# First feed-forward product: the third of a group's seven products ahead of the second, one weight quarter loaded at another place, activations behind the next cast

## The chip, the cores and the metric

The kernel runs on one core of one Trainium2 chip. The metric is the device time of one execution in microseconds (us). The profiler records one execution: what every engine did and when, in us from the first instruction.

## What is computed

The whole program is one block of a network: a projection of the input, two attention-like branches, a merge, a layer norm, a feed-forward part, a gate and a second layer norm, on 512 tokens of width 1024. The change touches the feed-forward part and the work just ahead of it:

```python
h = layer_norm(DEEPNORM_ALPHA * h + merged @ w_out[l], ln1_g[l], ln1_b[l])
ff = jnp.square(jax.nn.relu(h @ w_ff1[l])) @ w_ff2[l]          # w_ff1 1024 x 4096, w_ff2 4096 x 1024
r = DEEPNORM_ALPHA * h + ff
r = r + jax.nn.sigmoid(r @ w_ple_gate[l]) * (p[l] @ w_ple_proj[l])
h = layer_norm(r, ln2_g[l], ln2_b[l])
```

## The kernel before, in words

**The first feed-forward product** (`h @ w_ff1`) is cut into four groups of 1024 columns, in the order `groups = (2, 3, 0, 1)`; t counts them 0 to 3. In a group, h is a 2 x 2 block matrix (two halves of the tokens, two of the width) and the weights are the four quarters B11, B12, B21, B22 of 512 x 512. A group's eight block products are replaced by seven products P1 to P7 of sums of blocks, after Strassen and Winograd. The sums of h blocks are made once, as tiles `hc0` to `hc6`; the rows of TensorE (PE) name a product by its tile: P1 is hc0, P2 is hc1, P3 is hc6, P4 is hc2, P5 is hc3, P6 is hc4, P7 is hc5. A product is 48 matmuls of 128 x 256: each fp32 operand is split into a high and a low part (`w1h` and `w1l` for the weights), and high by high, high by low and low by high are added up.

**The sums of weight quarters** are made in place. `w1_load` brings a quarter from HBM into a tile `w1q` (issued by SP). `w1_factor` casts the quarter to `w1h` on ScalarE (ACT) and takes the rest to `w1l` on VectorE (DVE), in two halves of 128 x 1024. Behind each half of P1, P5 and P3 it issues, from GpSimd (POOL), a transfer that adds another quarter to this half in place (`accum_op=OP.add`, L887). So there are three pairs of such adding transfers in a group:

- the **P1 pair**, behind the split of B11 for P1: adds B12 to B11. P5 uses the sum.
- the **P3 pair**, behind the split of B22 for P3: adds B12 to B22. P7 uses the sum.
- the **P5 pair**, behind the split of B11 for P5: adds B22 to B11. P6 uses the sum, and DVE adds it to B21 for P4 (`w1q<-w1q`).

**The order.** `seq` lists the steps (group, product). At step k the code first splits the weights of step k+1 (`w1_factor`), then takes the result of step k-1 out of its PSUM banks (`ff1_sums`), and then issues the matmuls of step k (`ff1`, L958). In steps with `late_` the sums come ahead of the split. `queued` keeps the ACT and DVE instructions of these parts in the order of the code, and `issue_after` does so for the matmuls. Splits write into two buffers by turns, so the split for step k+1 waits until the matmuls of step k-1 have read theirs.

**Results.** `ff1_sums` copies or adds PSUM banks into four tiles C00, C01, C10, C11 (`c` in the rows), and `act` squares the ReLU of a finished one on ACT, in two instructions, into `uLH` or `uH`; C11's is one DVE instruction (`last_act`). The finished tiles of the first two groups are stored to DRAM (`spill`, issued by SP) and read back later. `w1_banks` says which two PSUM banks a product uses: `sets[0]` or `sets[3]`, by the group's parity, for P1 and P6; `sets[1]` for P2 and P5; `sets[2]` for P3, P7 and P4. P6 adds onto P1's bank and P4 onto P7's; P3 and P7 start fresh, so the one waits until the sums have read what P4 left there, the other until they have read P3.

**Places.** Quarters B11 and B22 lie in four places w80 to w83 that hold other things before. B22 of group 0 goes into w83, B22 of group 1 into w82, B11 of group 1 into w80. Before that, w82 and w83 hold the two halves of `w_ple_proj` (tile `wp`), which `ple_projection` reads in eight small products (`ppw`, stored through `pws` to `pwd`), the four of the first half (hh = 0) first. These stand on PE directly ahead of P1 of group 0.

**After it** comes the second feed-forward product (`ff2`, L1188), built in the same way, then the gate and the last norm.

Of the kernel before, what the change touches and what calls it, by code (L numbers as in the profile page):

```python
# [50 lines left out]
def f(ap):  # L51
    return ap.bitcast(F32)
# [3 lines left out]
def block_kernel(ctx: ExitStack, tc: tile.TileContext, t, out):  # L56
    nc = tc.nc
    te, ve, se, ge, sy = nc.tensor, nc.vector, nc.scalar, nc.gpsimd, nc.sync
# [22 lines left out]
    def acc(name):  # L81
        return ps_pool.tile([P, 512], F32, tag="acc", bufs=3, name=name)

    def aux(name):
        return ps_pool.tile([P, 512], F32, tag="aux", bufs=1, name=name)

    def misc(name):
        return ps_pool.tile([P, 512], F32, tag="misc", bufs=4, name=name)
# [14 lines left out]
    def gtile(name, dtype=F32R, n=None):  # L103

        if n is None:
            n = len(gplaces) % 4
            gplaces.append(n)
        return gpool.tile([P, 4, S], dtype, tag=f"g{n}", bufs=1, name=name)


    def split(src, hi, lo, lo_eng=None):
        se.copy(hi, src)
        low(lo_eng or ve, lo, src, hi)
# [11 lines left out]
    def raw_tile(shape, name):  # L125
        return rawpool.tile(shape, F32, tag="wr", bufs=3, name=name)
# [20 lines left out]
    def chunked(src):  # L147
        return src.rearrange("(k p) c -> p k c", p=P)
# [187 lines left out]
    for i in range(1, NT):  # L336
        n = (i + 1) * P
# [325 lines left out]
    def place(name, shape, dtype, n=None, pl=None):  # L663

        if n is None:
            n = len(places) % 4
            places.append(n)
        return (pl or w2).tile(shape, dtype, tag=f"w8{n}", bufs=1, name=name)

    def load_half(src, k, hh, name, lo_eng=None, pl=None, n=None):  # L670

        raw = raw_tile([P, 2, 512], name + "r")
        sy.dma_start(raw, chunked(src[k * 256:(k + 1) * 256, hh * 512:(hh + 1) * 512]))
        w = place(name, [P, 2, 2, 512], F32R, n, pl)
        split(raw, w[:, 0], w[:, 1], lo_eng)
        return w[:, 0], w[:, 1]
# [73 lines left out]
    def half_product(ps, sh, sl, ws):  # L750

        for k, (wh, wl) in enumerate(ws):
            mm = mm3(ps, sh(k), sl(k), wh, wl, k == 0, k == len(ws) - 1)
        return mm

    def blocks(ws):
        return [(wh[:, k, :], wl[:, k, :]) for wh, wl in ws for k in range(2)]
# [37 lines left out]
    def ple_inputs():  # L795
        prw = ln.tile([P, NT, PLE], F32, name="prw")
        sy.dma_start(prw, p_d.rearrange("(i p) c -> p i c", p=P))
        pT = place("pT", [P, 2, 2, S], F32R, 0)
        pTH, pTL = pT[:, 0], pT[:, 1]
        for c in range(2):  # L800
            ps = (aux, acc)[c]("pps")
            for i in range(NT):
                te.transpose(ps[:, i * P:(i + 1) * P], prw[:, i, c * P:(c + 1) * P], ident)
            split(ps, pTH[:, c, :], pTL[:, c, :])
        wp = [load_half(t["w_ple_proj"][0], 0, hh, "wp", (ge, ve)[hh], None, 2 + hh) for hh in range(2)]
        return pTH, pTL, wp

    w_ff1, w_ff2 = t["w_ff1"][0], t["w_ff2"][0]
# [2 lines left out]
    def queued(engine, op, *args, **kw):  # L811

        if engine in order_of:
            with tc.issue_after(order_of[engine].ins):
                order_of[engine] = getattr(engine, op)(*args, **kw)  # L815
        else:
            order_of[engine] = getattr(engine, op)(*args, **kw)
# [26 lines left out]
    pTH, pTL, wp = ple_inputs()  # L844
# [5 lines left out]
    P1, P2, P3, P4, P5, P6, P7 = range(7)  # L850
    B11, B12, B21, B22 = (0, 0), (0, 1), (1, 0), (1, 1)
    groups = (2, 3, 0, 1)
    w1q, pools = {}, {}

    def w1_rows(t, w):
        c = groups[t] * 1024 + w[1] * 512
        return w_ff1[w[0] * 512:(w[0] + 1) * 512, c:c + 512].rearrange("(k p) c -> p k c", p=P)

    def w1_load(t, w):

        if t >= len(groups):
            return
        e = (t + 1) % 2
        if w == B21:
            tl = pools[e].tile([P, 4, 512], F32, tag=f"x{e}", bufs=1, name="w1q")
        else:
            tl = place("w1q", [P, 4, 512], F32, (0 if w == B11 else 2) + e)
        w1q[t, w] = tl
        if loads:
            with tc.issue_after(loads[-1].ins):  # L870
                loads.append(sy.dma_start(tl, w1_rows(t, w)))
        else:
            loads.append(sy.dma_start(tl, w1_rows(t, w)))
# [5 lines left out]
    def w1_factor(t, n):  # L879

        tl = w1q[t, W1_OF[n]]
        hi, lo = (pools[1].tile([P, 4, 512], F32R, tag="w1" + x, bufs=2, name="w1" + x) for x in "hl")
        for k in (slice(0, 2), slice(2, 4)):
            queued(se, "copy", hi[:, k], tl[:, k])
            queued(ve, "tensor_sub", lo[:, k], tl[:, k], f(hi[:, k]))
            if n in W1_ADD:
                ge.dma_start(out=tl[:, k], in_=w1_rows(t, W1_ADD[n])[:, k], accum_op=OP.add)  # L887
        if n == P6:
            for k in (slice(0, 2), slice(2, 4)):
                queued(ve, "tensor_add", w1q[t, B21][:, k], w1q[t, B21][:, k], tl[:, k])  # L890
        return hi, lo
# [11 lines left out]
    def ple_projection(i, hh):  # L903
        ps = acc("ppw")
        tok = slice(i * P, (i + 1) * P)
        projected[:] = [half_product(ps, lambda k: pTH[:, k, tok], lambda k: pTL[:, k, tok], blocks(wp[hh:hh + 1]))]
        if i == 0:
            pwss.append(gtile("pws", F32))
        pws = pwss[hh][:, i]
        stored[:] = [se.copy(pws, ps)]  # L910
        sy.dma_start(pwd[:, i, hh * 512:(hh + 1) * 512], pws)

    todo = [(i, hh) for hh in range(2) for i in range(NT)]
    for _ in range(4):
        ple_projection(*todo.pop(0))
    with tc.issue_after(normed[0].ins), tc.issue_after(stored[0].ins):
        w1 = w1_factor(0, P1)

# [18 lines left out]
    sets = [[acc("pf"), acc("pf")], [acc("pf"), aux("pf")], [misc("pf"), misc("pf")], [misc("pf"), misc("pf")]]  # L937
    HALF = {P1: A11, P2: A12, P3: S4, P4: A22, P5: S1, P6: S2, P7: S3}

    def w1_banks(t, n):  # L940
        return sets[{P1: t % 2 * 3, P6: t % 2 * 3, P2: 1, P5: 1}.get(n, 2)]

    mms = []

# [93 lines left out]
    def add(g, tl, w):  # L1038
        return ge.dma_start(out=tl, in_=rows_of(g, w), accum_op=OP.add)  # L1039

    def factor(pl, src, kind, width, bufs=1, own=None):
        shape = [P, 4, width]
        hi, lo = own or (pl.tile(shape, F32R, tag=kind + x, bufs=bufs, name=kind + x) for x in "hl")
        split(src, hi, lo)
        return hi, lo
# [3 lines left out]
    def group_acts(g, which=(0, 1)):  # L1049

        for c in which:
            acts[g, c] = gtile("uLH"[0:3:c + 1], F32, 2 * (g % 2) + c)
            views[g, c] = acts[g, c].rearrange("p (a b) (c q) -> p a (b c) q", a=2, c=2)

    views, quarters = {}, {}
    seq = [(t_, n) for t_ in range(len(groups)) for n in (P1, P2, P3, P5, P7, P6, P4)]
    for k, (t_, n) in enumerate(seq):
        if n == P1:
            group_acts(groups[t_])
            if t_ == 0:  # L1060
                for w in (B22, B11, B22, B21):
                    w1_load(0 if (0, B22) not in w1q else 1, w)
        last = seq[k - 1] if k else None

        late_ = n in (P5, P7, P6)
        if late_:
            ff1_sums(*last)
        if k + 1 < len(seq):
            nxt = w1_factor(*seq[k + 1])
        if n == P7 and t_ == 3:  # L1070

            own = [place("w" + x, [P, 4, 512], F32R, 3 - k_) for k_, x in enumerate("hl")]
            queued(se, "copy", own[0], quarters[0, B11])
            queued(ve, "tensor_sub", own[1], quarters[0, B11], f(own[0]))
            begun = [own]
            add(0, quarters[0, B11], B12)
        if last and not late_:
            ff1_sums(*last)
        if n == P7:
            w1_load(t_ + 2, B22)  # L1080
        elif n == P6:
            w1_load(t_ + 2, B11)
            if t_ > 1:
                with tc.issue_after(loads[-1].ins):
                    load(t_ - 2, B11)
        elif n == P4:
            w1_load(t_ + 2, B21)
        elif n == P3 and t_ in (1, 2):
            for c in range(2):
                sy.dma_start(spilled[groups[t_ - 1]][:, c], views[groups[t_ - 1], c])  # L1090
        elif n == P5 and t_ == 3:
            xa = pools[1].tile([P, 2, 4, 256], F32R, tag="x1", bufs=1, name="xa")
            begun_a = factor(None, views[0, 0][:, 0], "a", 256, own=(xa[:, 0], xa[:, 1]))
        ff1(t_, n, w1)
        w1 = nxt
# [289 lines left out]
```

## Time and profile before

| | us |
|---|---|
| median of 3 runs | 786.79 (785.26 to 787.12) |
| the profiled execution, its own time | 787.04 |
| its span, first to last instruction | 785.3 |
| PE busy in the span | 761.5 |
| start of the first feed-forward product on PE | 413.12 |

1.74 us of the profiled execution's time lie outside its span. A term worked out from the trace is taken off 787.04, which is 0.25 us above the median of the runs.

### The profile page before, as it was taken

How to read it: one execution, taken by the hardware profiler on the slowest of the kernel's cores; microseconds unless marked ns; L12 is line 12 of the kernel's file. 1: busy time of each engine (PE TensorE's matmuls, PEld its weight loads, DVE VectorE, ACT ScalarE, POOL GpSimd, SP SyncE). 2: the span in 40 equal slices, each digit the busy share in tenths (PEclk: the TensorE clock that was granted, in tenths of full speed). 3: DMA queues.
4: the chain of work that ended last, by engine and by line, in shares of the span. 5: the costliest groups of instructions: out<-in, count | busy, mean ns of one | idle time of the engine just before them, and what ended most of it. 6: DMA issues, size and time to landing. Idle time of an engine off the chain costs nothing.

```text
span 785.3 us, 11629 instructions
## 1 busy us (share of the span) xinstructions
PE 761.5 (97%) x4374; PEld 662.7 (84%) x4374; DVE 586.6 (75%) x983; ACT 419.0 (53%) x639; POOL 281.5 (36%) x356
## 2 busy tenths in 40 slices
PE   8999999999999999999999899989999999999995
PEld 8888888779988888877888899989988888888885
DVE  4668999974549996375796575757689989898458
ACT  4545566777747552343174665656665555656221
POOL 4745554433245446568332020211211101126341
PEclk9999999999999999999999999999999999999998
DMA  7424133222132202456149888764698799895302
GB/s 224 144 81 108 55 81 89 60 81 54 55 81 81 67 15 68 126 186 225 50 152 325 177 210 206 216 153 107 109 230 206 139 374 328 154 184 180 108 28 107
DMA packets 80434, 110.43 MB, mean 141 GB/s; under 512 B 5749, under 2 KB 42101, under 8 KB 79098
## 3 DMA queue, kind: packets, MB, share of 16 engines
q1 hardware_dynamic: 63754, 76.14, 29.6%
q0 software_dynamic: 13920, 27.27, 20.0%
q10 hardware_dynamic: 2704, 6.29, 2.4%
q8 instruction: 34, 0.56, 0.3%
q14 instruction: 22, 0.18, 0.1%
HBM read 101.29 MB, written 8.39 MB: 140 GB/s over the span
## 4 chain that ended last, share of the span: by engine, by line
PE 59%; DVE 16%; DMA 10%; issue 6%; POOL 5%; ACT 3%; SPq 0%; DVEq 0%; POOLq 0%; ACTq 0%
PE pf L1188 19%; DMA w1q<-in_w_ff 7%; PE pf L958 7%; DVE sc L361 3%; DVE m L360 3%; DMA wor<-in_w_out 2%; PE pg L151 2%; PE pg L153 2%; PE pg L152 2%; POOL aqwl L144 1%; PE pu L151 1%; PE pu L153 1%; PE pu L152 1%; DVE sc L351 1%; POOL w1q L887 1%
## 5 line engine op out<-in xcount | busy, mean ns | idle before, releaser
L815 DVE TENSOR_TENSOR w1l<-w1q,w1h 128x1024 fp32r<-128x1024 f32 x55 | 65.2, 1221 | 53.4 <-ACT w1h L815 52.5
L815 ACT CAST w1h<-w1q 128x1024 fp32r<-128x1024 f32 x55 | 55.8, 1050 | 32.7 <-DMA w1q<-in_w_ff 23.2
L887 POOL DMA_DIRECT2D w1q<-in_w_ff x24 | 29.2, 1254 | 120.5 <-DVE w1l L815 104.5
L815 DVE TENSOR_TENSOR wl<-b,wh 128x2048 fp32r<-128x2048 f32 x28 | 64.7, 2310 | 9.3 <-ACT wh L815 9.3
L144 POOL TENSOR_TENSOR wgl<-wgr,wgh 128x256 fp32r<-128x256 f32 x64 | 50.8, 827 | 47.9 <-ACT wgh L141 39.9
L1039 POOL DMA_DIRECT2D b<-in_w_ff x14 | 17.9, 1279 | 130.8 <-DVE wl L815 99.9
L1188 PE MATMUL pf<-wh,ah 128*128 128x512 f32 x216 | 58.1, 391 | 0.2 <-ACT wh L815 0.2
L1188 PE MATMUL pf<-wh,al 128*128 128x512 f32 x216 | 57.8, 389 | 0.0
L815 ACT CAST wh<-b 128x2048 fp32r<-128x2048 f32 x28 | 53.4, 1908 | 3.6 <-DMA b<-in_w_ff 3.6
L1188 PE MATMUL pf<-wl,ah 128*128 128x512 f32 x216 | 53.5, 390 | 0.0
L153 PE MATMUL pg<-xH,wgl 128*128 128x512 f32 x128 | 50.7, 396 | 0.0
L152 PE MATMUL pg<-xL,wgh 128*128 128x512 f32 x128 | 50.6, 395 | 0.0
L151 PE MATMUL pg<-xH,wgh 128*128 128x512 f32 x128 | 50.3, 393 | 0.0
L1188 PEld LDWEIGHTS pf<-wh,ah 128*128 128x128 f32 x216 | 40.3, 188 | 8.9 <-ACT wh L815 0.7
L1188 PEld LDWEIGHTS pf<-wh,al 128*128 128x128 f32 x216 | 40.5, 188 | 8.5
L1188 PEld LDWEIGHTS pf<-wl,ah 128*128 128x128 f32 x216 | 40.5, 188 | 8.4
L144 POOL TENSOR_TENSOR wul<-wur,wuh 128x128 fp32r<-128x128 f32 x64 | 34.3, 568 | 19.0 <-ACT wuh L141 17.2
L815 ACT ACTIVATE c<-c 128x1024 f32<-128x1024 f32 x12 | 12.7, 1062 | 33.8 <-DVE c L815 33.8
L815 DVE TENSOR_TENSOR c<-c,pf 128x512 f32<-128x512 f32 x48 | 30.4, 678 | 0.0
L152 PEld LDWEIGHTS pg<-xL,wgh 128*128 128x128 f32 x128 | 24.0, 188 | 4.5
L151 PEld LDWEIGHTS pg<-xH,wgh 128*128 128x128 f32 x128 | 24.1, 188 | 4.4
L153 PEld LDWEIGHTS pg<-xH,wgl 128*128 128x128 f32 x128 | 24.1, 188 | 4.3
(404 smaller groups left out, 2312.4 us busy)
## 6 DMA issues: line engine op xcount, KB each, us to landing
b<-in_w_ff POOLq DMA_DIRECT2D x14, 1024.0 KB, 9.5
w1q<-in_w_ff SPq DMA_DIRECT2D x12, 1024.0 KB, 5.5
w1q<-in_w_ff POOLq DMA_DIRECT2D x24, 512.0 KB, 9.0
wgr<-in_w_in SPq DMA_DIRECT2D x16, 512.0 KB, 3.8
b<-in_w_ff SPq DMA_DIRECT2D x8, 1024.0 KB, 6.8
wor<-in_w_out SPq DMA_DIRECT2D x8, 512.0 KB, 5.4
b<-in_w_ff ACTq DMA_DIRECT2D x4, 1024.0 KB, 12.1
wpgr<-in_w_ple_gate SPq DMA_DIRECT2D x8, 512.0 KB, 10.2
```

The source lines that it names most:

```text
L144: (lo_eng or ge).tensor_sub(lo[:, k:k + n], raw[:, k:k + n], f(hi[:, k:k + n]))
L151: te.matmul(ps, sh, mh, start=first, stop=False, **kw)
L152: te.matmul(ps, sh, ml, start=False, stop=False, **kw)
L153: return te.matmul(ps, sl, mh, start=False, stop=last, **kw)
L351: ve.scalar_tensor_tensor(sc, rl, wi[:, i, h:h + 1], sc, op0=OP.mult, op1=OP.add)
L360: ve.max(m8, sc)
L361: ve.match_replace(out=sc, in_to_replace=m8, in_values=sc, imm_value=NEG_TAKEN)
L815: order_of[engine] = getattr(engine, op)(*args, **kw)
L887: ge.dma_start(out=tl[:, k], in_=w1_rows(t, W1_ADD[n])[:, k], accum_op=OP.add)
L958: mm = te.matmul(ps, w[:, k, b * P:(b + 1) * P], a[:, k], start=fresh, stop=w is lo and k == 3, skip_group_check=True)
L1039: return ge.dma_start(out=tl, in_=rows_of(g, w), accum_op=OP.add)
L1188: mm = te.matmul(banks[n, s], (al if kind == 1 else ah)[:, q, tok], (wl if kind == 2 else wh)[:, q], start=fresh and kind == 0 and q == 0, ...
```

## The change

In groups 1 to 3 the products are done in the order P1, P3, P2, P5, P7, P6, P4; group 0 keeps P1, P2, P3. P5 is no longer one of the steps with the sums ahead of the split. P2 of groups 1 to 3 uses the set of banks that P1 of the group before used. B22 of group 0 is loaded behind the first four `ple_projection` calls, and to that end the two halves of `wp` change places, so that the half that is read first lies in w83. The stores of finished tiles stand one step later in the code.

```diff
-        wp = [load_half(t["w_ple_proj"][0], 0, hh, "wp", (ge, ve)[hh], None, 2 + hh) for hh in range(2)]
+        wp = [load_half(t["w_ple_proj"][0], 0, hh, "wp", (ge, ve)[hh], None, 3 - hh) for hh in range(2)]
...
     for _ in range(4):
         ple_projection(*todo.pop(0))
+    w1_load(0, B22)
     with tc.issue_after(normed[0].ins), tc.issue_after(stored[0].ins):
         w1 = w1_factor(0, P1)
...
     def w1_banks(t, n):
-        return sets[{P1: t % 2 * 3, P6: t % 2 * 3, P2: 1, P5: 1}.get(n, 2)]
+        e = t % 2 * 3
+        return sets[{P1: e, P6: e, P2: 3 - e if t else 1, P5: 1}.get(n, 2)]
...
-    seq = [(t_, n) for t_ in range(len(groups)) for n in (P1, P2, P3, P5, P7, P6, P4)]
+    seq = [(t_, n) for t_ in range(len(groups)) for n in ((P1, P3, P2) if t_ else (P1, P2, P3)) + (P5, P7, P6, P4)]
     for k, (t_, n) in enumerate(seq):
         if n == P1:
             group_acts(groups[t_])
             if t_ == 0:
-                for w in (B22, B11, B22, B21):
-                    w1_load(0 if (0, B22) not in w1q else 1, w)
+                for w in (B11, B22, B21):
+                    w1_load(1, w)
         last = seq[k - 1] if k else None
-        late_ = n in (P5, P7, P6)
+        late_ = n in (P7, P6)
...
-        elif n == P3 and t_ in (1, 2):
+        elif n == P5 and t_ in (1, 2):
             for c in range(2):
                 sy.dma_start(spilled[groups[t_ - 1]][:, c], views[groups[t_ - 1], c])
```

SP's queue ahead of group 0, before (-) and after (+). `w1q_4563` (before) and `w1q_4467` (after) are B22 of group 0, `w1q_4565` is B11 and `w1q_4567` B22 of group 1:

```order
 L871 DMA w1q_4401<-in_w_ff1 128x4x512
-L911 DMA pwd_4017<-pws_4437 128x512 x4
-L911 DMA pwd_4017<-pws_4484 128x512 x2
-L871 DMA w1q_4563<-in_w_ff1 128x4x512
-L911 DMA pwd_4017<-pws_4484 128x512 x2
+L911 DMA pwd_4017<-pws_4437 128x512 x3
+L871 DMA w1q_4467<-in_w_ff1 128x4x512
+L911 DMA pwd_4017<-pws_4437 128x512
+L911 DMA pwd_4017<-pws_4486 128x512 x2
 L871 DMA w1q_4565<-in_w_ff1 128x4x512
```

The load of B22 moved ahead of four of the stores of `pws`; the stores of the finished tiles (`spill`) stand in this queue between the same loads as before.

ACT in group 0, from the cast for P3 on; first before. `w1q_4563` and `w1q_4467` are B22 (casts for P3 and P7), `w1q_4369` is B11 (casts for P5 and P6):

```order
L815 CAST w1h_4625<-w1q_4563 128x1024 x2
L815 COPY c00_4549<-pf_4553 128x512
L815 COPY c00_4549<-pf_4554 128x512
L815 CAST w1h_4683<-w1q_4369 128x1024 x2
L815 ACTIVATE c00_4549<-c00_4549 128x1024
L815 ACTIVATE uLH_4561<-c00_4549 128x1024
L815 COPY c01_4550<-pf_4557 128x512
L815 COPY c01_4550<-pf_4558 128x512
L815 CAST w1h_4745<-w1q_4563 128x1024 x2
L815 COPY c11_4552<-pf_4555 128x512
L815 COPY c11_4552<-pf_4556 128x512
L815 CAST w1h_4803<-w1q_4369 128x1024 x2
```

The same place after the change:

```order
L815 CAST w1h_4625<-w1q_4467 128x1024 x2
L815 COPY c00_4551<-pf_4555 128x512
L815 COPY c00_4551<-pf_4556 128x512
L815 CAST w1h_4683<-w1q_4369 128x1024 x2
L815 ACTIVATE c00_4551<-c00_4551 128x1024
L815 ACTIVATE uLH_4563<-c00_4551 128x1024
L815 CAST w1h_4743<-w1q_4467 128x1024 x2
L815 COPY c01_4552<-pf_4559 128x512
L815 COPY c01_4552<-pf_4560 128x512
L815 COPY c11_4554<-pf_4557 128x512
L815 COPY c11_4554<-pf_4558 128x512
L815 CAST w1h_4803<-w1q_4369 128x1024 x2
```

The copies of C01, which empty the banks of P3, stood ahead of the cast for P7 and now stand behind it.

DVE in group 1, from the split for the second product on; first before. `w1q_4569` is B21 (for P2), `w1q_4567` B22 (for P3 and P7), `w1q_4565` B11 (for P5):

```order
L815 TENSOR_TENSOR w1l_4988<-w1q_4569,w1h_4987 128x1024 x2
L815 TENSOR_TENSOR c10_4551<-c10_4551,pf_4557 128x512
L815 TENSOR_TENSOR c10_4551<-c10_4551,pf_4558 128x512
L815 TENSOR_TENSOR w1l_5046<-w1q_4567,w1h_5045 128x1024 x2
L815 SCALAR_TENSOR_TENSOR uH_4562<-c11_4552 128x1024
L815 TENSOR_TENSOR w1l_5105<-w1q_4565,w1h_5104 128x1024 x2
L815 TENSOR_TENSOR c00_4549<-c00_4549,pf_4555 128x512
L815 TENSOR_TENSOR c00_4549<-c00_4549,pf_4556 128x512
L815 TENSOR_TENSOR w1l_5169<-w1q_4567,w1h_5168 128x1024 x2
```

The same place after the change:

```order
L815 TENSOR_TENSOR w1l_4988<-w1q_4567,w1h_4987 128x1024 x2
L815 TENSOR_TENSOR c10_4553<-c10_4553,pf_4559 128x512
L815 TENSOR_TENSOR c10_4553<-c10_4553,pf_4560 128x512
L815 TENSOR_TENSOR w1l_5048<-w1q_4569,w1h_5047 128x1024 x2
L815 SCALAR_TENSOR_TENSOR uH_4564<-c11_4554 128x1024
L815 TENSOR_TENSOR w1l_5105<-w1q_4565,w1h_5104 128x1024 x2
L815 TENSOR_TENSOR w1l_5163<-w1q_4567,w1h_5162 128x1024 x2
L815 TENSOR_TENSOR c00_4551<-c00_4551,pf_4555 128x512
L815 TENSOR_TENSOR c00_4551<-c00_4551,pf_4556 128x512
```

The splits of B22 for P3 and of B21 for P2 changed places, and the split for P7 moved ahead of the adds that empty the banks of P2. The split for P5 stands where it stood. `c10` is the sum that empties P4 of the group before.

## Rows read from the trace of the kernel before

**Rows 1.** The page: the span, and PE's busy time.

```profile
span 785.3 us, 11629 instructions
PE 761.5 (97%) x4374; PEld 662.7 (84%) x4374; DVE 586.6 (75%) x983; ACT 419.0 (53%) x639; POOL 281.5 (36%) x356
```

**Rows 2.** PE's waits from 405 to 585 us: who waited for whom, us in total, times, longest. From 565 us to the end the second row is the only one.

```profile
PE pf L958 <- ACT w1h L815: 7.3, 5, 2.2
PE pf L1188 <- ACT wh L815: 0.2, 1, 0.2
```

**Rows 3.** PE in order of time: start, duration, instruction, count, and in brackets the idle time ahead of it and what ended it. The first rows of P1 of group 0, P3, P7 (two rows) and P6 of group 0, P1 and P7 and P6 and P4 of group 1, P1 and P7 (two rows) of group 2, P1 of group 3, and the first row of the second feed-forward product, which stands ahead of P4 of group 3.

```profile
413.12 0.63 PE L958 MATMUL pf<-hc0H,w1h 128*128 128x256 f32 x4
...
425.62 0.50 PE L958 MATMUL pf<-hc6H,w1h 128*128 128x256 f32 x2 [1.45 <-ACT w1h L815]
...
437.35 0.46 PE L958 MATMUL pf<-hc5H,w1h 128*128 128x256 f32 x2
439.96 0.50 PE L958 MATMUL pf<-hc5H,w1h 128*128 128x256 f32 x2 [2.15 <-ACT w1h L815]
...
445.30 0.62 PE L958 MATMUL pf<-hc4H,w1h 128*128 128x256 f32 x4
...
456.18 0.62 PE L958 MATMUL pf<-hc0H,w1h 128*128 128x256 f32 x4
...
477.94 0.39 PE L958 MATMUL pf<-hc5H,w1h 128*128 128x256 f32 x2
...
484.71 0.94 PE L958 MATMUL pf<-hc4H,w1h 128*128 128x256 f32 x4
...
490.47 0.62 PE L958 MATMUL pf<-hc2H,w1h 128*128 128x256 f32 x4
...
495.91 0.62 PE L958 MATMUL pf<-hc0H,w1h 128*128 128x256 f32 x4
...
517.67 0.39 PE L958 MATMUL pf<-hc5H,w1h 128*128 128x256 f32 x2
520.28 0.50 PE L958 MATMUL pf<-hc5H,w1h 128*128 128x256 f32 x2 [2.22 <-ACT w1h L815]
...
538.11 0.62 PE L958 MATMUL pf<-hc0H,w1h 128*128 128x256 f32 x4
...
570.75 3.89 PE L1188 MATMUL pf<-wh,xa 128*128 128x512 f32 x16
```

**Rows 4.** Group 1 in order of time on DVE, POOL, SP's queue and ACT: the split for the second product and the sum of the P4 before, the split for the third product, the P3 pair and the P5 pair, a store of a finished tile, and the casts for P7 (second half) and P6 (second half). The rows at 501.00 and 524.22 are those of 460.88 and 484.05 one group later.

```profile
458.60 2.36 DVE L815 TENSOR_TENSOR w1l<-w1q,w1h 128x1024 fp32r<-128x1024 f32 x2 [1.97 <-ACT w1h L815]
460.88 1.28 DVE L815 TENSOR_TENSOR c<-c,pf 128x512 f32<-128x512 f32 x2
...
465.31 2.36 DVE L815 TENSOR_TENSOR w1l<-w1q,w1h 128x1024 fp32r<-128x1024 f32 x2 [3.16 <-ACT w1h L815]
...
501.00 1.27 DVE L815 TENSOR_TENSOR c<-c,pf 128x512 f32<-128x512 f32 x2
...
467.14 2.42 POOL L887 DMA_DIRECT2D w1q<-in_w_ff  x2 [11.31 <-issue]
470.31 2.42 POOL L887 DMA_DIRECT2D w1q<-in_w_ff  x2 [0.75 <-DVE w1l L815]
...
464.37 0.34 SPq L1090 DMA_DIRECT2D spill<-uLH  x1
...
478.29 1.04 ACT L815 CAST w1h<-w1q 128x1024 fp32r<-128x1024 f32 x1 [1.92 <-DMA w1q<-in_w_ff]
...
484.05 1.05 ACT L815 CAST w1h<-w1q 128x1024 fp32r<-128x1024 f32 x1 [1.31 <-DMA w1q<-in_w_ff]
...
524.22 1.05 ACT L815 CAST w1h<-w1q 128x1024 fp32r<-128x1024 f32 x1 [1.47 <-DMA w1q<-in_w_ff]
```

**Rows 5.** Group 0 in order of time: ACT's copy of the fourth small projection, SP's load of B22, the cast for P3, the P3 pair's issue, and the second halves of the casts for P7 and P6.

```profile
406.70 0.59 ACT L910 COPY pws<-ppw 128x512 f32<-128x512 f32 x1 [0.61 <-PE ppw L153]
...
413.31 0.99 SPq L871 DMA_DIRECT2D w1q<-in_w_ff  x1
...
424.53 1.99 ACT L815 CAST w1h<-w1q 128x1024 fp32r<-128x1024 f32 x2 [7.00 <-DMA w1q<-in_w_ff]
...
427.13 2.41 POOL L887 DMA_DIRECT2D w1q<-in_w_ff  x2 [14.67 <-DVE w1l L815]
...
438.86 1.04 ACT L815 CAST w1h<-w1q 128x1024 fp32r<-128x1024 f32 x1 [1.61 <-DMA w1q<-in_w_ff]
...
443.92 1.05 ACT L815 CAST w1h<-w1q 128x1024 fp32r<-128x1024 f32 x1 [1.50 <-DMA w1q<-in_w_ff]
```

**Rows 6.** Stretches: length, busy us (and instructions) of PE, PEld, DVE, ACT, POOL, then the granted clock of TensorE, the mean busy share of the 16 DMA engines and the GB/s that they moved.

```profile
409.00:411.00 2.00, 2.00 (x14) 1.76 (x13) 2.00 (x3) 2.00 (x4) 1.17 (x2) 1.00 0.00 0
420.00:431.00 11.00, 9.10 (x77) 8.70 (x77) 4.89 (x5) 4.86 (x6) 3.40 (x3) 1.00 1.04 391
431.00:441.00 10.00, 7.85 (x69) 7.64 (x68) 3.31 (x4) 6.15 (x8) 1.40 (x2) 1.00 1.13 213
462.00:465.00 3.00, 3.00 (x29) 3.00 (x28) 0.16 (x1) 2.78 (x3) 0.00 (x0) 1.00 0.01 1
469.00:485.00 16.00, 14.95 (x131) 14.64 (x129) 8.15 (x9) 8.14 (x11) 2.97 (x3) 1.00 1.08 251
521.00:523.00 2.00, 2.00 (x13) 2.00 (x12) 1.89 (x4) 1.25 (x2) 0.00 (x0) 0.56 0.87 159
```

## The prediction

> **What bounds the kernel now.** I read the page first: PE is busy 761.5 of 785.3 us [rows 1], so time can come back only where PE waits, or where it runs slowly. Next PE's waits in the stage of the change: one line, 7.3 us in five waits, for the cast `w1h` on ACT; afterwards there is only one wait of 0.2 us [rows 2]. The second feed-forward product and what follows keep PE full, and their transfers are started by places that PE sets free, so that part should follow PE when the first product ends earlier.
>
> Then PE in order of time [rows 3]. A product without a wait takes 5.44 us (P4 of group 1, 490.47 to 495.91), a group of seven 38.08. The groups took 43.06, 39.73, 42.20 us (from one P1 row to the next), and group 3 lost nothing: six products end at 538.11 + 32.64 = 570.75. So the stage lost 4.98 + 1.65 + 4.12 = 10.75 us, more than the waits, since a clock fall is in it. By place:
>
> - Group 0: P3 was due at 413.12 + 10.88 = 424.00, and everything from there stood 2.47 us late by P7 (437.35 instead of 434.88). P7 cost 2.51 more (P6 at 445.30 instead of 442.79).
> - Group 1: P6 began 1.33 us late behind P7's wait (484.71 instead of 477.94 + 5.44 = 483.38), and P6 itself cost 0.32.
> - Group 2: all 4.12 are at P7: 2.22 us of idle time, and then matmuls at the lower clock; the granted share is 0.56 from 521 to 523 us [rows 6], most of the time at 1.2 instead of 2.4 GHz.
>
> What ended last in each? P3 of group 0 waited for its quarter B22: loaded from 413.31 on, it landed at 424.53, 11.2 us later [rows 5]. P7 waited for the P3 pair. In group 1 the split for P3 began on DVE at 465.31, the pair was issued from 467.14 on, and its second half landed at 478.29, when P7 had been due at 477.94 [rows 4]. P6 stands just behind: the second half of the P5 pair landed at 484.05. The DMA engines are the reason for slow landings: full from 469 to 485 us (share 1.08), yet idle from 462 to 465 (0.01) [rows 6].
>
> **The change, part by part.** No engine gets another instruction or loses one; only places change.
>
> *P3 ahead of P2, groups 1 to 3.* The split for P3 takes the place of the split for P2: 458.60 in group 1 instead of 465.31 [rows 4], so the P3 pair is issued 6.7 us earlier, from 460.4 on. Even with the slowest flight in the group (P5 pair, issue at 470.31, second issue some 1.2 later, landing at 484.05: 12.5 us) its second half would land near 461.6 + 12.5 = 474.1, 3.8 us ahead of P7's due time. P7's wait goes: 1.33 in group 1, 4.12 with the clock fall in group 2. The split for P2 gets the old time of P3's, and B21 was loaded a group earlier, so it costs nothing.
>
> *What is late next: P6.* With P7 on time P6 is due at 483.38, and the second half of the P5 pair, whose cast takes 1.05, must land by 482.3, 1.7 us earlier than now. Its issue does not move (the split for P5 keeps its place), but the engines do. A pair moves 1.05 MB at 213 GB/s, the rate from 431 to 441 [rows 6], so 4.9 us. From 462 to 469 the engines had one store to do (464.37 [rows 4]; 1.05 MB at 391 GB/s are 2.7 us), so 4.3 us of the P3 pair fit there, and the P5 pair would land near 479.8. Against it: the next load of B22 is set free by P7's split, which now comes earlier, and it may put 2.7 us of its own ahead: 482.5. So P6 waits 0 to 0.2 us in group 1; by the same sum in group 2 (524.22 becomes 519.9 to 522.6, needed by 517.67 + 5.44 - 1.05 = 522.06) 0 to 0.5. I leave 0.1 and 0.3: gains of 1.55 and 3.8.
>
> *The bank of P3.* P3 now begins one product, not two, after P4 of the group before, and in the same banks. They are set free by the sum of P4 on DVE, which stands behind the split for the second product. Half of it was done at 460.88 + 0.64 = 461.52, and P3 is due at 456.18 + 5.44 = 461.62: just in time. In group 2 it is 501.64 against 501.35, so 0.3 late. Between nothing and 3 x 0.3 I charge 0.2, since most of that lateness came from the late P5 pair of the group before.
>
> *B22 of group 0 loaded earlier.* The fourth small projection is out at 406.70 [rows 5], so the load starts there, 6.6 us earlier than at 413.31, into engines that stood idle from 409 to 411 [rows 6]. Even after 11.2 us it is there at 417.9, and P3's split can start when P1 leaves its buffer (413.12 + 5.44 = 418.56). P3's 2.47 us go. The P3 pair is then issued near 418.6 + 1.8 = 420.4 (split to issue took 1.83 in group 1), not 427.13.
>
> *But group 0 is bound by the engines.* They are full from 420 to 441 [rows 6], and all that the change takes out of this stretch is B22's own 2.7 us. So the last half of the P5 pair lands near 443.92 - 2.7 = 441.2, its cast ends at 442.3, and P6 begins near 442.1 instead of 445.30: 3.2 gained. If the three loads of group 1 go ahead of the P3 pair, that pair lands at 438.86 - 2.7 = 436.2; the cast and, by the new order on ACT, the copy of C01 behind it (0.59, as the copy at 406.70 [rows 5]) put P7 at 437.8 and P6 at 443.2: 2.1 gained. If the next load of B22, set free by P7, comes wholly ahead of the P5 pair, P6 begins at 444.9: 0.4. At most all 4.98 return. I take 2.4, between the two likely values.
>
> The Trainium skill (DMA: Bandwidth & Descriptors, section Queues, rings and completion order) says that each DMA engine goes round robin over its queues, a packet at a time. By that the P3 pair would take its share beside the loads from 420 on and land well ahead of P7, and the sum would use 3.2 (778.5 us). The rows point the other way without deciding it: the pair issued at 427.13 found the engines moving 391 GB/s up to 431 and 213 only after that, and with the loads first the sum would use 2.1 (779.6).
>
> *At nothing:* the `wp` halves (their casts exchange places; the half that is read first comes one cast later, on PE's full queue); the P2 bank (read six products before); the store of finished tiles (same place in SP's queue); `act` of C00 and the sum of P2 behind P7's cast and split (read by nobody before the store in the next group; if the cast is late, so is P7 anyway). The second product's wait of 0.2 goes with the earlier P5 pair.
>
> **Sum:** 2.4 + 1.55 + 3.8 + 0.2 - 0.2 = 7.75 us off the profiled execution's 787.04: 779.3. Bounds: 4.98 + 1.65 + 4.12 + 0.2 = 10.95, so 776.1, and the first rival's 782.7.
>
> **The rivals.**
>
> - *The wait moves to P6.* If the P5 pair lands as late as now, P6 of group 1 begins at 484.05 + 1.05 = 485.1, no gain there, and in group 2 at 525.3 instead of 523.11, 2.2 of 4.12 lost. 2.4 + 0 + 1.9 = 4.3, so 782.7. For it: the engines are full to 485. Against: the idle stretch from 462 to 465 takes up work. A clock fall that stays, or comes elsewhere, gives some 781.
> - *No wait left*, in group 0 too: 776.1. Against: 2.7 us is all that its engines are spared.
> - *The change does not do it:* the P3 pair, issued earlier, lands no earlier because the engines give it no time. Then only group 0 gains: 787.04 - 2.4 = 784.6. The 3 idle us speak against it.
> - *Slower: P3's bank.* If DVE reached the sum of P4 only behind the split for the third product (it ends at 465.31 + 2.36 = 467.67), P3 would begin at 468.3 instead of 461.62, 6.7 us in three groups: 779.3 + 20 = 799. The listed order puts the sum ahead of that split, so DVE would have to be late. It decides from 2.6 us per group on (7.75 / 3), that is when the sum's first half ends 8 us after P1's start, where it is now 5.3 to 5.7.
>
> **How the numbers follow.** Forecast (777.5 to 781.5) 0.62; wait at P6, 0.14; no wait left, 0.13; does not do it, 0.06; bank, 0.05. The range goes from 776.0 to 782.7 and leaves out the last two cases. 0.3% or 2.4 us is about what a measurement of this kernel can tell from no change. The first three cases are faster (0.88, some of the tail given up); "does not do it" lies on the border and gives most of 0.07; the bank gives 0.05.
>
> **What would show it.** Right: in groups 1 and 2 no wait ahead of P7, the P3 pair issued some 4.3 us behind P1's start, engines busy where 462 to 465 was idle; P3 of group 0 at 424.0, P6 of group 0 near 442; the second product begins 7 to 8 us earlier, and from there on all is shifted alike. Wrong: a wait of over half a us ahead of P6 in groups 1 to 3, a wait of PE for DVE's `c` ahead of P3, a clock fall, or time lost again after 570 us.

## The result, and the profile after

The changed kernel takes 781.85 us (median of 14 runs, 778.19 to 784.26), the kernel before 786.61 beside it: a ratio of 0.9931, 95% interval 0.9914 to 0.9948. The forecast was 779.3 with a range of 776.0 to 782.7. So the gain has the sign and about the size that was forecast, but the runs of the changed kernel spread over 6 us, where those of before spread over 3.6, and the profiled execution is the slowest of them, 784.26. Why that is so is the main thing to be learned here.

The page of the changed kernel: span, busy time by engine, and the granted clock in 40 slices.

```profile
span 782.5 us, 11627 instructions
PE 765.6 (98%) x4374; PEld 668.4 (85%) x4374; DVE 585.6 (75%) x983; ACT 418.4 (53%) x639; POOL 282.9 (36%) x356
PEclk9999999999999999999999999999999999999999
```

PE has the same 4374 matmuls as before and is busy 4.1 us longer [rows 1], at a granted clock of 0.9 or more in every slice. The matmuls themselves have become longer.

PE's waits from 405 to 585 us: one is left of the 7.5 us [rows 2], and from 560 us to the end there is none.

```profile
PE pf L960 <- ACT c L815: 0.6, 1, 0.6
```

PE in order of time: first rows of P1, P7 and P6 of group 0, then of all seven products of group 1 (P1, P3, P2, P5, P7, P6, P4), then of P1 of group 2.

```profile
414.99 0.64 PE L960 MATMUL pf<-hc0H,w1h 128*128 128x256 f32 x4
...
438.39 0.75 PE L960 MATMUL pf<-hc5H,w1h 128*128 128x256 f32 x4 [0.63 <-ACT c L815]
...
444.16 0.63 PE L960 MATMUL pf<-hc4H,w1h 128*128 128x256 f32 x4
...
455.47 0.63 PE L960 MATMUL pf<-hc0H,w1h 128*128 128x256 f32 x4
...
461.12 0.63 PE L960 MATMUL pf<-hc6H,w1h 128*128 128x256 f32 x4
...
466.77 0.64 PE L960 MATMUL pf<-hc1H,w1h 128*128 128x256 f32 x4
...
472.43 0.63 PE L960 MATMUL pf<-hc3H,w1h 128*128 128x256 f32 x4
...
478.08 0.63 PE L960 MATMUL pf<-hc5H,w1h 128*128 128x256 f32 x4
...
483.73 0.64 PE L960 MATMUL pf<-hc4H,w1h 128*128 128x256 f32 x4
...
489.39 0.63 PE L960 MATMUL pf<-hc2H,w1h 128*128 128x256 f32 x4
...
495.04 0.63 PE L960 MATMUL pf<-hc0H,w1h 128*128 128x256 f32 x4
```

Group 1 runs from product to product without a pause, and yet each step is 5.65 or 5.66 us, not 5.44 [rows 3]. Over 48 matmuls that is 117.8 ns from start to start in place of 113.3. The rows of single instructions say the same. Matmuls of P2's first kind (count, and duration in ns: least, median, most), before and then after:

```profile
L958 PE MATMUL pf<-hc1H,w1h x64: 276/276/277, 418.6 to 546.6; 128*128 128x256 f32 x64
```

```profile
L960 PE MATMUL pf<-hc1H,w1h x64: 280/281/282, 420.6 to 549.1; 128*128 128x256 f32 x64
```

These matmuls have **two paces**, and in a timeline the eye finds them at once: four matmuls are 0.62 us long at the one and 0.63 or 0.64 at the other. All 27 products ahead of P4 of group 3 ran at 113.3 ns in the trace of before (away from its waits and its clock fall), and all at 117.8 ns in this one. The granted clock is 1.00 at both. The 128x512 matmuls of the second feed-forward product stood at 226.7 ns (24 of them in 5.44 us) in traces of either kind.

Counted from the first P1 to the interlude of 128x512 matmuls ahead of the last P4, the two executions compare as follows. Waits are what is left of the stretch when 27 products at the trace's own pace are taken off.

| us | before | after | difference |
|---|---|---|---|
| start of P1 of group 0 | 413.12 | 414.99 | +1.87 |
| 27 products at the trace's pace | 146.9 | 152.7 | +5.8 |
| waits and what follows from them | 10.7 | 0.85 | -9.9 |
| from the interlude to the end | 216.29 | 215.73 | -0.56 |
| whole execution | 787.04 | 784.26 | -2.78 |

The waits went even more completely than forecast (9.9 for 7.75), the pace took 5.8 back, and 1.87 were lost ahead of the stage. That last term varies from one execution to the next: P1 of group 0 began at 412.45 us when the same kernel was profiled again (after_again), and at 415.94 us in late_all, which is the same kernel up to there. Part of it is work further ahead: in the first trace PE waited 1.8 us for the weight tile `wo` (1.4 in after_again), and the granted clock from 350 to 412 us was 0.97 (1.00 in after_again).

What should show each step does show. The P3 pair and the P5 pair of group 1 as POOL issued them, then ACT's casts for P7 and for P6, each in one row of two halves:

```profile
459.00 2.42 POOL L887 DMA_DIRECT2D w1q<-in_w_ff  x2 [4.35 <-DVE w1l L815]
469.12 2.42 POOL L887 DMA_DIRECT2D w1q<-in_w_ff  x2 [7.70 <-DVE w1l L815]
...
470.74 2.00 ACT L815 CAST w1h<-w1q 128x1024 fp32r<-128x1024 f32 x2 [1.88 <-PE pf L960]
...
479.27 2.00 ACT L815 CAST w1h<-w1q 128x1024 fp32r<-128x1024 f32 x2
```

Neither cast waits for a DMA any more: the one for P7 waits for PE to leave its buffer, the one for P6 for nothing [rows 4]. The idle stretch of the DMA engines is filled and the clock fall in group 2 is gone [rows 6]; columns as there:

```profile
462.00:465.00 3.00, 3.00 (x27) 3.00 (x27) 0.88 (x1) 2.97 (x5) 0.00 (x0) 1.00 1.10 196
469.00:485.00 16.00, 16.00 (x138) 16.00 (x137) 10.37 (x12) 8.02 (x9) 2.42 (x2) 1.00 0.73 202
521.00:523.00 2.00, 2.00 (x19) 2.00 (x19) 2.00 (x3) 0.00 (x0) 0.00 (x0) 1.00 0.03 8
```

### The profile page after: what moved, and what is told of

Read it like the earlier page. It is cut to its first block, busy times and chain, and to the rows that moved or that the text cites. A ratio compares the mean times of both kernels' runs of the same rounds, so it can differ in the third digit from the quotient of the medians.

```text
span 782.5 us, 11627 instructions
## 1 busy us (share of the span) xinstructions
PE 765.6 (98%) x4374; PEld 668.4 (85%) x4374; DVE 585.6 (75%) x983; ACT 418.4 (53%) x639; POOL 282.9 (36%) x356
## 4 chain that ended last, share of the span: by engine, by line
PE 73%; DVE 15%; POOL 3%; issue 3%; DMA 2%; ACT 2%; SPq 1%; DVEq 0%; POOLq 0%; ACTq 0%
PE pf L960 20%; PE pf L1191 19%; DVE sc L361 3%; DVE m L360 3%; PE po L152 2%; PE po L153 2%; PE po L151 2%; PE pg L151 2%; PE pg L153 2%; PE pg L152 2%; POOL aqwl L144 1%; PE pu L151 1%; PE pu L153 1%; PE pu L152 1%; DVE sc L351 1%
```

## The experiments

Medians below are of runs on one chip within each part, beside the kernel before there. Only one execution of each set has a trace; which pace the others had is inferred from their times.

### Whose pace is it?

Three theories: **A**, the pace is drawn anew in each execution, or stretch of it, whatever the kernel; **B**, the slower pace belongs to the new order or its banks; **C**, the time was lost ahead of the stage. Four kernels, with before at 785.82 us: each of the two again, the new order alone, and the early load alone.

> The changed kernel, unaltered, profiled once more. In its first trace a product of the first feed-forward stage took 5.66 us where it took 5.44 before, with the same matmuls, no wait and a granted clock of 1.00; 27 products make 6 us of it. Theory A (the pace is drawn anew in each execution): this trace shows products at 5.44 in at least one long stretch or in all, and the timed runs spread over 778 to 784.5 us. Theory B (the new order or the new banks bring the slower pace): again 5.66 in all 27 products ahead of the interlude of the second product, runs at 782 to 785. Theory C (the time was lost ahead of the stage): products at 5.44, P1 of group 0 near 415 again.

> The kernel before, unaltered, profiled once more. Theory A: some stretch of the stage between two waits may run at 5.66 a product here too; since the waits are for transfers, a slower PE then waits less, and the total moves by 2 to 3 us at most (785 to 789). Theory B: 5.44 in all products, 785 to 787.5, the waits ahead of P3 and P7 as in the first trace.

The two halves of the change, as they stand in the kernels:

```diff
order_only: the kernel before, with
...
+        return sets[{P1: e, P6: e, P2: 3 - e if t else 1, P5: 1}.get(n, 2)]
...
+    seq = [(t_, n) for t_ in range(len(groups)) for n in ((P1, P3, P2) if t_ else (P1, P2, P3)) + (P5, P7, P6, P4)]
...
+        late_ = n in (P7, P6)
...
+        elif n == P5 and t_ in (1, 2):
load_only: the kernel before, with
+        wp = [load_half(t["w_ple_proj"][0], 0, hh, "wp", (ge, ve)[hh], None, 3 - hh) for hh in range(2)]
...
+    w1_load(0, B22)
...
+                for w in (B11, B22, B21):
+                    w1_load(1, w)
```

> The kernel before with the new order, the new banks of P2, the sums of the step before P5 behind the split, and the stores a step later; the load of B22 of group 0 and the places of wp stay as before. At the pace of 5.44 the prediction gives 1.55 + 3.8 - 0.2 for groups 1 and 2, so 781 to 782, with P3 and P7 of group 0 still late by 2 to 3 us each. Theory A: up to 6 us on top where the slower pace is drawn (781 to 788). Theory B: 5.66 in every product behind P3 of group 0, 786 to 788.

> The kernel before with B22 of group 0 loaded behind the fourth small projection and the halves of wp exchanged, the order as before. The prediction gives 2.4 us (0.4 to 5.0) from group 0 and the waits of groups 1 and 2 unchanged, so 784 to 785. Theory A: either pace, with up to 2 to 3 us on top. Theory B: 5.44 in all products, since the order and the banks are those of before.

| | median us | ratio, 95% interval | profiled execution | pace of its 27 products |
|---|---|---|---|---|
| after_again | 783.28 | 0.9964 (0.9947 to 0.9980) | 781.00 | 8 at 113.3, then 117.8 |
| before_again | 786.50 | 1.0012 (0.9998 to 1.0026) | 787.39 | 117.8 but for P3 and P5 of group 0 |
| order_only | 783.00 | 0.9980 (0.9958 to 1.0001) | 780.68 | P1 and P2 of group 0 at 117.8, the rest 113.3 |
| load_only | 782.95 | 0.9964 (0.9950 to 0.9978) | 783.30 | 5 at 117.8, then 113.3 |

A holds; B falls, and so does C, whose products at 5.44 did not come back with a P1 near 415 (after_again has P1 at 412.45 and 19 products at the slower pace). The kernel before, unchanged, shows the slower pace (P1's rows, all four groups):

```profile
L958 PE MATMUL pf<-hc0H,w1h x64: 280/281/281, 413.2 to 540.9; 128*128 128x256 f32 x64
```

and the new order shows the faster one (P1 of groups 1, 2 and 3 in order_only, 38.08 us apart, which is seven times 5.44: not a tenth of a microsecond is lost in groups 1 and 2):

```profile
456.18 0.62 PE L959 MATMUL pf<-hc0H,w1h 128*128 128x256 f32 x4
...
494.26 0.62 PE L959 MATMUL pf<-hc0H,w1h 128*128 128x256 f32 x4
...
532.34 0.62 PE L959 MATMUL pf<-hc0H,w1h 128*128 128x256 f32 x4
```

In after_again the pace changes at P3 of group 1, which began some 0.3 us late. P1 in its faster rows, then P3's first two:

```profile
455.23 0.62 PE L960 MATMUL pf<-hc0L,w1h 128*128 128x256 f32 x4
455.68 1.98 PE L960 MATMUL pf<-hc0H,w1l 128*128 128x256 f32 x16
457.79 0.71 PE L960 MATMUL pf<-hc6H,w1h 128*128 128x256 f32 x4
458.33 0.64 PE L960 MATMUL pf<-hc6L,w1h 128*128 128x256 f32 x4
```

Why before takes nearly the same time at either pace stands in before_again's waits of the stage:

```profile
PE pf L958 <- ACT w1h L815: 5.0, 4, 2.2
```

7.3 us of waiting for `w1h` became 5.0. The transfers set the time, and a PE that is slower arrives later and waits less; in group 2 the wait shrinks from 2.2 to 0.4 us. 787.39 us at the slower pace, 787.04 at the faster. Where the waits are gone, the pace is paid in full: 27 x 0.215 = 5.8 us. The runs of order_only lie in two heaps, 780.68 to 784.11 (eight) and 786.84 to 787.77 (four). Of the changed kernel's 32 runs in three sets, seven end below 779.7 and twenty between 782.5 and 784.4.

Load_only alone gained 2.9 us of 785.82; the sum had 2.4 for group 0, and the 784 to 785 of its forecast were missed. In its trace the time from P1 of group 0 to P1 of group 1 is 39.42 us, against 43.06 before, though five of the seven products ran at the slower pace.

### Can the pace be set?

P4 of group 3, right behind sixteen matmuls of 128x512, had stood at 113.4 to 113.6 ns in all six traces up to here. So wide matmuls were put ahead of P1. The `ff1` of wide1 (wide4: four; wide16: sixteen, in group 0 alone):

```diff
         ah, al = hcH[HALF[n]], hcL[HALF[n]]
+
+        def wide():
+            mms.append(te.matmul(w1_banks(t, n)[0][:, :512], hi[:, 0, :P], ah[:, 0:2], start=True, stop=True,
+                                 skip_group_check=True))
+
+        for _ in range(1 if n == P1 else 0):
...
+                wide()
```

> The changed kernel with one more matmul of 128x512 ahead of P1 in each of the four groups, into the bank that P1 then starts fresh, so its result is thrown away. It costs 4 x 0.23 = 0.9 us. Theory W1, wide matmuls set the faster pace (P4 of group 3, right behind sixteen of 128x512, stood at 113.3 to 113.6 ns in six traces of six): each P1 is at 113.3 ns, and the time is the changed kernel's fastest, 778.6, + 0.9 = 779.5, in nearly all runs. Theory W2, any disturbance draws the pace anew: four more draws in an execution, so P1 rows at either pace, times spread from 779.5 to 785, median 782 to 783. Theory W3, one disturbance does nothing: P1 of groups 1 to 3 keep the pace of the P4 before them, times as the changed kernel's (median 783.3) + 0.9 = 784.2.

> As wide1, with four matmuls of 128x512 ahead of each P1: 16 x 0.23 = 3.6 us. W1: P1 rows at 113.3 ns, 778.6 + 3.6 = 782.2 in nearly all runs. W2: either pace, 782 to 788. W3: the pace of the P4 before, median 783.3 + 3.6 = 786.9.

> Sixteen matmuls of 128x512 ahead of P1 of group 0 alone, as many as stand ahead of P4 of group 3: 3.6 us. W1: P1 of group 0 at 113.3 ns, and since a pace has held until the next disturbance, most of the stage too: 782.2 in most runs. W2: P1 of group 0 at 113.3 ns in some executions only, times in two heaps near 782 and 787.

Before stood at 786.16 here. Wide1: 781.52 us (779.68 to 782.26), ratio 0.9938 (0.9924 to 0.9953). Wide4: 781.41 (780.30 to 783.43), 0.9942 (0.9928 to 0.9956). Wide16: 785.46, 0.9974 (0.9952 to 0.9997), in two heaps, three runs from 779.22 to 779.44 and nine from 784.54 to 787.41. In the traces P1 of the four groups stands at 113.4, 117.8, 117.8, 113.4 ns in wide1 and at 117.8, 113.4, 113.4, 113.4 in wide4. In wide4 four rows show the switch: the wide matmuls and the low part of P5, of groups 0 and 1:

```profile
412.60 1.10 PE L953 MATMUL pf<-hc0H,w1h 128*128 128x512 f32 x4
434.26 2.05 PE L971 MATMUL pf<-hc3H,w1l 128*128 128x256 f32 x16
453.68 1.10 PE L953 MATMUL pf<-hc0H,w1h 128*128 128x512 f32 x4
474.57 1.98 PE L971 MATMUL pf<-hc3H,w1l 128*128 128x256 f32 x16
```

W2 holds: a break draws anew, at about even odds (with the kernel called best below, 7 of 13 P1s behind such a break, in the four kernels that have one, were at the faster pace). W3 falls, since P1 takes another pace than the P4 ahead of it (in seven of the nine P1s that have a P4 ahead; so few do not show whether a draw depends on the pace before it). W1 falls with the slow P1s, and in wide16 even P4 of group 3 stood at 117.8. The runs of wide1 agree: four draws in each execution, and both extremes are gone from its times. The medians of wide1 and wide4 came out below W2's figures, too (from 782 up for both). A forecast missed: wide16's faster heap was expected at 782.2 and lies at 779.4, so most of its 3.6 us was hidden. Why stays open; in after_again, whose group 0 ran at the faster pace, P7 of group 0 waited 1.2 us for work behind a late transfer, which may be part of it, and in wide16's own trace, at the slower pace, PE waits for nothing in the stage.

Three times a pace changed without any pause that the waits show: load_only's P6 of group 0, wide1's P3 of group 1, late_all's P7 of group 0. What decides a draw stays open.

### The waits that are left

After the change ACT copies C01 behind the cast for P7 in group 0. In late_all the sums stand ahead of the split at P5 again:

```diff
-        late_ = n in (P7, P6)
+        late_ = n in (P5, P7, P6)
```

> The changed kernel with P5 again one of the steps with the sums ahead of the split, so that the copy of C01 stands ahead of the cast for P7 in group 0, and in groups 1 to 3 the sum of P2 and the squares of C00 stand ahead of it. Theory L, the only wait left is this copy's: PE's wait of 0.6 us ahead of P7 of group 0 goes, no other comes, since in groups 1 to 3 the cast for P7 has a whole product to spare; P6 of group 0 then waits for its own cast, so 0.3 us are gained, 783.0. Rival M, the squares ahead of the cast make P7 late in groups 1 to 3: 2.1 us of ACT each, a wait of up to 1 us in each, 785.

782.07 us (778.85 to 784.99), 0.9944 (0.9923 to 0.9965), beside the same 786.16. Its only wait of the stage is the one that theory L names, P6 of group 0 for its own cast; none in groups 1 to 3, which ran at 117.8 ns there, so M falls at that pace:

```profile
445.03 0.50 PE L960 MATMUL pf<-hc4H,w1h 128*128 128x256 f32 x2 [0.44 <-ACT w1h L815]
```

The 0.3 us at stake are below what the spread of the pace lets a run show, and the order does not always gain them: in best (below), which also copies C01 ahead of the cast and ran group 0 at 113.3 ns, P7 and P6 waited 2.0 us together, against 1.2 in after_again. This part of the change is worth nothing that can be measured.

The other three stand beside the changed kernel (after_third) with before at 786.75 us. Bank_late makes the slower rival real:

```diff
+        if n == P3 and t_:
+            ff1_sums(*seq[k - 2])
-        if last and not late_:
+        if last and not late_ and n != P1:
             ff1_sums(*last)
```

> The slower rival made real: in groups 1 to 3 the sum of P4 of the group before stands on DVE behind the split for the third product of the group instead of ahead of it. By the changed kernel's trace that split ran in group 1 from 464.12 to 466.48, so the first half of the sum would end near 467.1 and P3, due at 461.1, would begin near 467.2: 6.1 us in each of three groups, 783.3 + 18 = 801 (797 to 804, a fall of the granted clock behind the idle time not counted). If the bank of P3 were not what P3 needs, or another wait stood behind it already, nothing or less: 783 to 790.

796.10 us (793.38 to 799.02), 1.0135 (1.0113 to 1.0157): 12.8 above the changed kernel's 783.27. DVE in group 1 (the split for the third product, then the sum of P4), and P3's first rows of groups 1 and 2:

```profile
459.50 2.36 DVE L815 TENSOR_TENSOR w1l<-w1q,w1h 128x1024 fp32r<-128x1024 f32 x2 [0.55 <-issue]
461.77 1.28 DVE L815 TENSOR_TENSOR c<-c,pf 128x512 f32<-128x512 f32 x2
...
462.60 0.71 PE L960 MATMUL pf<-hc6H,w1h 128*128 128x256 f32 x4 [3.20 <-DVE c L815]
...
505.61 1.11 PE L960 MATMUL pf<-hc6H,w1h 128*128 128x256 f32 x4 [3.20 <-DVE c L815]
```

The stretch behind the last of these rows:

```profile
506.00:510.00 4.00, 4.00 (x24) 4.00 (x23) 1.20 (x2) 3.08 (x4) 0.00 (x0) 0.61 0.89 271
```

The mechanism is as the rival had it, and the forecast of 797 to 804 was too high, because the wait is half as long: 3.2 us a group, not 6.1 or 6.7. The split began at 459.50, not 464.12, because its cast no longer stood behind the squares that wait for this same sum. In groups 2 and 3 a clock fall follows the wait (granted 0.61 from 506 to 510, between the levels of 1.2 and 2.4 GHz): P3 took 7.1 us in both, 1.7 more than 5.44. 3 x 3.2 + 2 x 1.7 = 13.0.

P4first goes the other way, and best adds to it the wide matmul and the copy of C01 ahead of the cast:

```diff
         elif n == P4:
-            add((1, 0))
-            if t < len(groups) - 1:
+            if t == len(groups) - 1:
+                add((1, 0))
+            else:
                 act(g, 1, 0)
...
+        if n == P1 and t_:
+            for b in range(2):
+                o = C[1, 0][:, 2 * b:2 * b + 2]
+                queued(ve, "tensor_add", o, o, w1_banks(*last)[b].rearrange("p (a b) -> p a b", a=2))
         if k + 1 < len(seq):
```

> The changed kernel with the sum of P4 ahead of the split for the second product of the next group, so that P3's bank is free 1.3 us after the group's start, not 5.5. Theory P, the bank costs P3 0.3 us where the matmuls run at 113.3 ns and nothing at 117.8 ns: no wait of PE for DVE's c ahead of P3, the split and the P3 pair 1.3 us later without a wait ahead of P7, and the time the changed kernel's within 0.3 us. Rival, the later split makes P3 itself wait for w1l: 0.5 us or more in each of three groups, 785.

> p4first, with one matmul of 128x512 ahead of each P1 (as wide1) and in group 0 the copy of C01 ahead of the cast for P7. By the draws seen so far (wide1 781.5, against 783.3 for the changed kernel on another chip call) and 0.3 to 0.5 us for the two waits: 781.0, 0.5 to 2 us below the changed kernel in this call; if the break of one wide matmul only draws anew at an even chance, 782 and no difference.

> The changed kernel unchanged, beside the other three on one chip: 781.5 to 783.5 in the median, spread from 778.2 to 784.4, most runs at the upper end.

P4first 780.79 us (778.12 to 784.21), 0.9929 (0.9904 to 0.9954); best 782.43 (780.71 to 782.58), 0.9942 (0.9928 to 0.9956); after_third 783.27 (778.68 to 783.99), 0.9949 (0.9928 to 0.9969). The intervals overlap, so neither is shown to beat the changed kernel, and best missed its 781.0 (its other figure, 782 if a break draws at an even chance, fits). P4first's rival falls: there is no wait ahead of P3 or P7 in groups 1 to 3, at 117.8 ns in p4first's trace, nor in group 2 of best's, which ran at 113.3 ns. Its own theory was not put to the test: the profiled execution stood at 117.8 ns from P7 of group 0 on, where the bank costs nothing anyway, and order_only paid nothing for the bank at 113.3 ns without this edit.

## Why the prediction was right, and where its sum was off

- **The waits of groups 1 and 2** (gains of 1.55 and 3.8): right, and slightly small. Nothing is left where 0.1 and 0.3 were left, in order_only at the forecast's own pace.
- **P6 late next:** right that it would not be. The P5 pair was put at 479.8 to 482.5; by 479.27 ACT took its first half without waiting for it, and the second half behind it likewise.
- **Group 0** (2.4, between 2.1 and 3.2): 1.1 us too small. In after_again, whose group 0 ran at 113.3 ns, the time from P1 of group 0 to P1 of group 1 is 39.60 us, not 43.06, so 3.5 were gained and 1.5 of the 4.98 lost are left. The case with loads first had the second half of the P3 pair at 436.2. ACT began the cast of that half at 434.02 there, its only wait being for the transfer, with P1 0.67 us earlier than before: 434.7. The copy of C01 stands behind that cast, and PE's wait for it, foreseen as 0.6 us, was 1.2 there and 0.6 in the first trace.
- **Which transfer goes first:** both cases hold in part. The two kinds of transfer go through two queues of the profile: SP's loads are its `hardware_dynamic`, POOL's adding transfers its `software_dynamic`. In after_again the P3 pair was issued from 419.91 on. From 420 to 424 us (first two lines; packets, MB, share of 16 engines) the loads had the engines alone, and from 424 to 434 us (last two) both moved side by side:

```profile
q1 hardware_dynamic: 830, 1.60, 104.8%
q0 software_dynamic: 4, 0.00, 0.6%
...
q0 software_dynamic: 642, 1.25, 67.3%
q1 hardware_dynamic: 707, 1.42, 41.8%
```

  The Trainium skill (DMA: Bandwidth & Descriptors, section Queues, rings and completion order) has each engine go round its queues by turns, a packet at a time. The trace agrees from 424 us on, with 642 and 707 packets, but not for the first 4 us behind the issue, in which the pair moved next to nothing; so it came at P7's due time (434.02 against 434.21) and not well ahead of it. The pair of before, issued at 427.13, shows the same: nothing up to 431 us. So the rate of 391 GB/s up to 431, which the prediction took for a sign of loads first, does not separate the two cases. What the 4 us are is not shown.
- **The bank of P3** (0.2): right in size. P3 of group 1 slipped by 0.3 us in after_again, of which 0.13 are a wait of PE for DVE's `c`, one of the signs named for a wrong forecast; in order_only, at the same pace, nothing was lost in three groups, and at 117.8 ns PE comes later and nothing is lost. The slower rival was priced at 6.7 us a group and costs 4.3 on average with its clock falls; the step that failed there took the split's start from a trace in which other work of ACT stood ahead of its cast.
- **No time lost after 570 us**, no clock fall in the stage: right. But the second product was to begin 7 to 8 us earlier, and began 2.2 earlier in the first trace (568.53 for 570.75) and 5.5 in after_again.
- **The step that was off: "a product without a wait takes 5.44 us".** It was read from an execution that stood at one pace throughout, and taken as a constant. At that pace the sum was 0.6 to 1.5 us too careful: of 10.7 of loss, 1.5 is left in group 0 (after_again) and between nothing (order_only) and three times 0.3 (after_again's one) at the bank, so 8.3 to 9.2 are gained and the time is 777.8 to 778.7; the changed kernel's fastest runs end at 778.2 to 778.8. At the other pace 5.8 us come on top and what is left of the loss shrinks to 0.85: 783.0, and most runs ended between 782.5 and 784.4. These figures keep the start of the stage at before's 413.12, which itself varies by some us. The median lies between the two, 2.5 us above the forecast. The range held it partly by luck: the waits went almost wholly (9.9 of 10.95), as in the rival without any wait left, and the slower pace, which nothing in the prediction allowed for, took much of that back. At the slower pace throughout the sum ends at 783.0, outside the range, and the medians of after_again and after_third (783.28 and 783.27) lie there too.

## What to carry to other kernels

A kernel that waits for transfers hides how fast its matmuls run; take the waits away and the gain is the waits less what the slower pace adds. So read the length of a stage without waits from more than one execution before it becomes the unit of a sum. More busy time at the same number of instructions and the same granted clock is the sign to look for. And the price of a wait that a reordering might bring cannot be read from the old queue, if what stood ahead of it moves too.

## What the runs showed of the hardware

Matmuls of 128x256, each with its own weight load, ran back to back at 113.3 or at 117.8 ns from start to start, at a granted clock of 1.00, with the weight loads at a median of 188 ns at both. From 546 to 564 us in the first traces the single steps lay at 112 to 114 ns in before and at 116 to 120 ns after the change. A pace lasts over hundreds of matmuls, is often changed by a break, and differs between executions of one program. Right behind sixteen matmuls of 128x512, in P4 of group 3, the faster one was seen in 11 of 14 traces. What sets the pace is not shown. Adding transfers issued by POOL while SP's loads kept the 16 engines full moved next to nothing for 4 us (420 to 424 us of after_again, 427 to 431 of before), and then 1.25 MB beside 1.42 MB of loads from 424 to 434 us.
